# A fused hybrid decoder layer on one core: two of four input-weight sums of the second feed-forward made in DRAM, all DRAM sums paced

## The chip, the cores and the metric

The kernel runs on one core of one Trainium2 chip. The metric is the device time of one launch in microseconds (us), the median of the runs shown. A core has five engines that run their own instruction streams in order and wait for each other by semaphores: TensorE (PE, matmuls), VectorE (DVE), ScalarE (ACT), GpSimd (POOL) and SyncE (SP, which here only issues transfers). Transfers are carried by 16 DMA engines; those that SP issues are in one queue (q1 in the profile), those that GpSimd issues, accumulating ones among them, in another (q0).

## The reference, cut to what matters

```
def reference(x, mem, ...):
    x = x + 0.5 * swiglu(rms_norm(x, norm_ffn1_w), ffn1_w_in, ffn1_w_out)
    x = x + hybrid_mixer(rms_norm(x, norm_mix_w), ...)      # SSD heads and differential attention
    x = x + memory_cross_attention(rms_norm(x, norm_cross_w), rms_norm(mem, norm_mem_w), ...)
    x = x + 0.5 * swiglu(rms_norm(x, norm_ffn2_w), ffn2_w_in, ffn2_w_out)
    return rms_norm(x, norm_final_w)

def swiglu(h, w_in, w_out):
    gate, up = split(h @ w_in, 2)
    return (silu(gate) * up) @ w_out
```

x is 512 tokens by 1024 features in float32, the feed-forward width is 2816 = 22 tiles of 128, the memory has 256 rows. Everything is float32.

## The kernel before

**Precision.** Each float32 operand is split into a high and a low part (`wh` on ScalarE by a copy, `wl` on VectorE by a subtraction, lines L151 and L152), and each product is three matmuls: high by high, high by low, low by high. The activations lie with features on partitions in the tiles `x[0..7]`.

**Block products.** Most of both feed-forwards is multiplied by a scheme of seven block products in place of eight (Winograd's form of Strassen's). It needs sums of blocks of the weights. `quad` makes two tiles each of gate and up outputs from four weight blocks of 128 x 1024 (512 KB), called b11, b12, b21, b22. It uses seven weight operands in this order: m1 = b11, t = b12 + b11, t2 = t + b22, m2 = b21, m7 = b12 + b22, m3 = b22, t4 = t2 + m2. Each of the seven is one call of `add_product`, 24 matmuls of 256 columns, into one of three accumulators in PSUM, named qa, qe and qb. Between products ScalarE copies accumulators (qb<-qa at L267, u<-qb at L277), and TensorE waits for these copies before it adds into qb again.

**How the sums are made.** In the first feed-forward VectorE adds t2 and t4 in SBUF. In the second one (`by_transfer`), SP loads a block into a raw tile `wr` and GpSimd issues a transfer that adds another block to it: t gets b11 from DRAM, t2 gets the finished tile t from SBUF, m7 gets b22 from DRAM. t4 is added by VectorE. The raw tiles have six buffers, the split ones three each.

**The output weights of the second feed-forward** are used in the same way by `out_blocks`: the work is cut into three parts (`THIRDS`: 8, 8 and 6 tiles of the width), each with its input quads (4, 4 and 3) and then seven block products into the accumulators oa, oe and ob, 24 or 18 matmuls of 512 columns each. Its four sums of blocks are made in DRAM, in the tensors `wsum`: SP copies a block to `wsum` (1 MB, or 768 KB for the last part), and GpSimd adds another one to it in slices of 512 KB. The generator `out_sums` issues this between the instructions of the mixer, 60 us of planned TensorE time after the first feed-forward ends.

**Order of the work.** The program is generated by Python generators: the dense matmuls run as one stream, and side work (attention heads, SSD groups, sums) is spawned as chains that become ready when a count of planned TensorE time (`od.t`) passes; `yield 5.0` means 5 us of it. SP's stream keeps this program order exactly. The streams of the other engines are ordered by a scheduler at build time. SP waits for a free `wr` buffer at each weight load, so its stream runs some five weight tiles ahead of TensorE.

**SSD groups.** Each of four groups (`group`) loads rows of cumulated decays, `r<-cum_d` (L790), by GpSimd, four of 256 KB; ScalarE and VectorE turn them into masked decays (L848 to L852), and TensorE multiplies them into `py`.

**The end.** After the last part's products, `update` adds them to the tiles x (now turned to tokens on partitions), and `final` makes the last norm: squares of both halves of a token block (junk, L1187), multiplication by the norm's weight (`gain`), a power on GpSimd (frr, L1193), a scaling, and two output transfers by SP. The norm's weight is loaded by SP ahead of the last part's output weights.

Of the kernel before, what the change touches and what calls it, by code (L numbers as in the profile page):

```python
# [11 lines left out]
F32 = mybir.dt.float32  # L12
R32 = mybir.dt.float32r
AF = mybir.ActivationFunctionType
ALU = mybir.AluOpType
# [81 lines left out]
def body(tc, a, dbg=None):  # L97
# [38 lines left out]
    last, start, last_sum, recent = [], [], [], []  # L136
# [111 lines left out]
    def quad(xs, src, by_transfer):  # L248

        b12, b11, b22, b21 = src[0], src[1], src[2], src[3]
        m1, t = raw_w(b11), raw_w(b12, b11)
        if by_transfer:
            t2, m2, m7, m3 = raw_w(b22, t), raw_w(b21), raw_w(b12, b22), raw_w(b22)
            t4 = m2
        else:  # L260
            m3, m2, m7 = raw_w(b22), raw_w(b21), raw_w(b12, b22)
# [5 lines left out]
        S.activation(b_ps, a_ps, AF.Copy)  # L267
# [3 lines left out]
        if not by_transfer:  # L271
            V.tensor_tensor(t2, t, m3, ALU.add)
        yield from add_product(b_ps, split_w(t2), xs, S2, False)
        if not by_transfer:
            V.tensor_tensor(t4, t2, m2, ALU.add)
        u2 = s2("u2")
        S.activation(u2, b_ps, AF.Copy)  # L277
# [123 lines left out]
    def ffn_quads(xs, wq, st, nq, made, places, by_transfer=False):  # L401

        for _ in range(nq):
            for out in quad(xs, next(wq), by_transfer):
                if out is None:
                    yield
# [372 lines left out]
    def group(g, bt, ct, xs, zs):  # L779
# [13 lines left out]


# [46 lines left out]
        for j in range(2):  # L841
# [235 lines left out]

    wsum = [[dram.tile([P, nf // 2 * T], F32, name=f"wsum{c}{t}") for t in range(4)] for c, (_, nf) in enumerate(THIRDS)]

    def out_sums():  # L1080
        for t, (to, of) in enumerate(((B12, B11), (B12, B22), (B22, 0), (B21, 2))):
            for c in range(len(THIRDS)):
                blocks = a[f"f2b{c}"]
                nc.sync.dma_start(wsum[c][t], blocks[to])
                yield 5.0
                more = wsum[c][of] if t > 1 else blocks[of]
                for k in range(0, more.shape[1], D):
                    ks = slice(k, min(k + D, more.shape[1]))
                    G.dma_start(wsum[c][t][:, ks], more[:, ks], accum_op=ALU.add)
                    yield 3.0  # L1090

    def out_blocks(c, g, col4, last):
# [37 lines left out]
        def update(tb, half_, src):  # L1130
            V.scalar_tensor_tensor(x[4 * half_ + tb], src, col4[:, tb : tb + 1], x[4 * half_ + tb], ALU.mult, ALU.add)  # L1131

# [35 lines left out]
        for t in range(2):  # L1168
            update(t, 1, e_ps[t])
            if last is not None:  # L1170
                last(t)
        for t, m in enumerate([product(b_ps, sums[3], "22", by_pair=last is not None)]):
            yield from m
        for t in range(2):
            update(t + 2, 0, b_ps[t])
            if last is not None:
                last(t + 2)

    def ffn2():
        wq = iter(a["f2q"])  # L1180
        col4, gain = None, []

        def final(tb):
            ss = small("fss", 2)
            for n in range(2):
                junk = s2("junk")
                S.activation(junk, x[4 * n + tb], AF.Square, accum_out=ss[:, n : n + 1])  # L1187
# [11 lines left out]
        for c, (_, nf) in enumerate(THIRDS):  # L1199
            g = []  # L1200
            yield from ffn_quads(xs_2, wq, st_2, nf // 2, block_tiles(g), BY_BLOCK, True)
# [102 lines left out]
```

## Time and profile before

| | |
|---|---|
| runs | 1382.34 us median of 3 (1377.25 to 1385.79) |
| the profiled execution | 1377.29 us, of which the instructions' span is 1375.3 us |
| granted TensorE clock | 0.985 mean |
| TensorE matmul busy | 1319.3 us (96%), 7766 recorded |
| VectorE, ScalarE, GpSimd busy | 978.0 us (71%), 667.3 us (49%), 135.0 us (10%) |
| moved | 211.17 MB; SP's queue 35.3% of the 16 engines' span, GpSimd's 20.4% |

Rough stages by time from the span's start: first feed-forward to 366 us, mixer to some 850 us, cross-attention to some 978 us, second feed-forward to the end. Its three parts have their quads at 978 to 1072, 1110 to 1199 and 1238 to 1311 us.

How to read it: a row of the timeline gives the start, the duration, engine, line, operation, tile written <- tiles read, and in square brackets the time that the engine stood idle before it and what ended that. In the table of waits the three numbers are the sum in us, the count and the longest. In the table by windows PEclk is the granted TensorE clock and DMA share the busy share of the 16 DMA engines.

### The profile page before, as it was taken

To read this page: it belongs to the slowest core of one execution; us is meant where nothing else is said; L and a number is where in the kernel's file an instruction comes from. 1 tells how busy PE (TensorE), PEld (TensorE's weight loads), DVE (VectorE), ACT (ScalarE), POOL (GpSimd) and SP (SyncE) were. 2 spreads that over 40 slices of the span, in tenths; PEclk is the share of its full clock that TensorE was granted. 3 is DMA by queue.
4 is the path that set the end of the run, shared out by engine and by line. 5 is a ranking of instruction groups with operands and counts; after the bars stand their busy time and mean duration, and the time that the engine had idled before them with its cause. 6 is when DMAs were issued, how large, how long until landed. Compare 5 with 4: busy or idle time off the path is not lost. (4 is left out here: it accounts for less than half of the span.)

```text
span 1375.3 us, 20006 instructions
## 1 busy us (share of the span) xinstructions
PE 1319.3 (96%) x7766; PEld 1145.8 (83%) x7766; DVE 978.0 (71%) x1533; ACT 667.3 (49%) x1124; POOL 135.0 (10%) x158
## 2 busy tenths in 40 slices
PE   8999999999999998999999999999999999999973
PEld 7888999799888787877888878888899899889862
DVE  6875778477875775657777786566978777876854
ACT  5442445155454563446654574344565544554543
POOL 1000010100122111200101110000110011001000
PEclk9999999999999999999999999999999999999987
DMA  7434576365489738721264473221677688768622
GB/s 262 109 121 123 132 205 237 90 175 151 142 287 242 211 85 160 239 91 55 37 149 85 102 182 114 92 63 55 144 189 209 199 230 200 199 191 238 186 76 84
DMA packets 62047, 211.17 MB, mean 154 GB/s; under 512 B 7880, under 2 KB 10416, under 8 KB 61760
## 3 DMA queue, kind: packets, MB, share of 16 engines
q1 hardware_dynamic: 47904, 162.62, 35.3%
q0 software_dynamic: 14048, 47.27, 20.4%
q8 instruction: 61, 1.00, 0.3%
q14 instruction: 34, 0.28, 0.1%
HBM read 201.94 MB, written 27.84 MB: 167 GB/s over the span
## 5 line engine op out<-in xcount | busy, mean ns | idle before, releaser
L151 ACT ACTIVATE wh<-wr 128x1024 fp32r<-128x1024 f32 (+2 forms) x311 | 316.0, 1020 | 378.2 <-issue 81.2
L152 DVE TENSOR_TENSOR wl<-wr,wh 128x1024 fp32r<-128x1024 f32 (+2 forms) x311 | 365.8, 1179 | 147.3 <-ACT wh L151 142.8
L142 PE MATMUL po<-gh,wh 128*128 128x512 f32 x176 | 68.8, 392 | 0.0
L142 PE MATMUL po<-gl,wh 128*128 128x512 f32 x176 | 68.5, 390 | 0.0
L142 PE MATMUL po<-gh,wl 128*128 128x512 f32 x176 | 68.4, 389 | 0.0
L231 PE MATMUL qa<-hmh,wl 128*128 128x256 f32 x216 | 61.2, 283 | 0.8 <-DVE wl L152 0.8
L231 PE MATMUL qa<-hml,wh 128*128 128x256 f32 x216 | 61.1, 283 | 0.0
L231 PE MATMUL qa<-hmh,wh 128*128 128x256 f32 x216 | 61.1, 283 | 0.0
L231 PE MATMUL qb<-s31h,wh 128*128 128x256 f32 x152 | 44.4, 292 | 8.4 <-ACT u L277 8.4
L142 PE MATMUL pxbc<-hnh,wh 128*128 128x512 f32 x128 | 52.3, 408 | 0.0
L142 PE MATMUL pxbc<-hnl,wh 128*128 128x512 f32 x128 | 50.2, 392 | 0.0
L142 PE MATMUL pxbc<-hnh,wl 128*128 128x512 f32 x128 | 50.2, 392 | 0.0
L666 ACT ACTIVATE ec<-ec,mn 128x512 f32<-128x512 f32 (+3 forms) x64 | 35.4, 555 | 29.3 <-DVE mn L665 29.3
L239 POOL DMA_DIRECT2D wr<-in_f2q x22 | 19.0, 862 | 295.3 <-DMA wr<-in_f2q 89.7
L231 PE MATMUL qb<-s24h,wh 128*128 128x256 f32 x152 | 44.4, 292 | 3.6 <-ACT qb L267 3.5
L231 PE MATMUL qe<-s31h,wh 128*128 128x256 f32 x152 | 44.0, 290 | 1.7 <-ACT wh L151 1.7
L231 PE MATMUL qe<-s31h,wl 128*128 128x256 f32 x152 | 43.8, 288 | 0.8 <-DVE wl L152 0.8
L231 PE MATMUL qe<-s31l,wh 128*128 128x256 f32 x152 | 43.9, 288 | 0.2 <-DVE s31l L152 0.2
L231 PE MATMUL qb<-s24l,wh 128*128 128x256 f32 x152 | 43.7, 288 | 0.0
L231 PE MATMUL qb<-s24h,wl 128*128 128x256 f32 x152 | 43.7, 287 | 0.0
L474 DVE TENSOR_TENSOR upd<-po,row 128x512 f32<-128x512 f32 x24 | 16.6, 690 | 38.1 <-PE po L142 38.0
L231 PE MATMUL qb<-s31h,wl 128*128 128x256 f32 x152 | 43.6, 287 | 0.0
(436 smaller groups left out, 4132.0 us busy)
## 6 DMA issues: line engine op xcount, KB each, us to landing
wr<-in_f2q SPq DMA_DIRECT2D x66, 512.0 KB, 4.8
wr<-in_f1q SPq DMA_DIRECT2D x40, 512.0 KB, 4.2
wr<-in_f2q POOLq DMA_DIRECT2D x22, 512.0 KB, 7.9
wr<-wsum SPq DMA_DIRECT2D x20, 512.0 KB, 4.2
wr<-in_f1q POOLq DMA_DIRECT2D x16, 512.0 KB, 5.9
wr<-in_f1o SPq DMA_DIRECT2D x16, 512.0 KB, 4.3
wr<-in_wxbc SPq DMA_DIRECT2D x16, 512.0 KB, 4.2
wr<-in_f2b SPq DMA_DIRECT2D x15, 512.0 KB, 3.9
```

What stands on the lines that cost most here:

```text
L142: nc.tensor.matmul(out, w, x, start=start, stop=stop)
L151: S.activation(hi, src, AF.Copy),
L152: V.tensor_tensor(lo, src, hi.bitcast(F32), ALU.subtract),
L231: nc.tensor.matmul(out, a_[:, wc], b_, start=first and f == 0 and kp == 0 and j == 0, stop=kp == n - 1 and j == 2, skip_group_check=True)
L239: last_sum[:] = [G.dma_start(raw, m, accum_op=ALU.add).ins]
L474: V.tensor_tensor(upd, po, row4, ALU.mult)
L666: S.activation(ec[:, :n], ec[:, :n], AF.Exp, bias=mn, scale=-1.0, accum_out=sm[c][:, i : i + 1])
```

## The change

Three things change.

1. For each of the 11 quads of the second feed-forward, t and t2 are made in DRAM (`isum`) during the mixer and cross-attention; `quad` loads them as it loads a plain block. Of the three adding transfers of a quad only m7's is left. The split of m7 and the addition of t4 change places in the code.
2. `block_sums_in_dram` takes the place of `out_sums`. It makes the sums of both kinds in one list of 46 jobs, part by part, in pieces of 512 KB: a copy by SP, and two jobs later the adding transfer by GpSimd, some 10 us of planned time a job, from 10 us after the first feed-forward. It issues nothing while a group stands in `hold`: from the group's start until its second pair of decay rows is in use.
3. The last norm is taken half by half: each update of a half is followed by that half's square and multiplication, and the second to come only adds. Its weight is loaded by GpSimd.

```
-    def quad(xs, src, by_transfer):
+    def quad(xs, src, ready):
...
-        m1, t = raw_w(b11), raw_w(b12, b11)
-        if by_transfer:
-            t2, m2, m7, m3 = raw_w(b22, t), raw_w(b21), raw_w(b12, b22), raw_w(b22)
+        m1 = raw_w(b11)
+        if ready:
+            t, t2, m2, m7, m3 = raw_w(ready[0]), raw_w(ready[1]), raw_w(b21), raw_w(b12, b22), raw_w(b22)
             t4 = m2
...
-        w2 = split_w(m2)
-        if by_transfer:
+        yield from add_product(a_ps, split_w(m2), xs, "12", False)
+        w7 = split_w(m7)
+        if ready:
             V.tensor_tensor(t4, t2, m2, ALU.add)
-        yield from add_product(a_ps, w2, xs, "12", False)
-        yield from add_product(b_ps, split_w(m7), xs, S3, False)
+        yield from add_product(b_ps, w7, xs, S3, False)
...
-            od.spawn(out_sums(), 60.0)
+            od.spawn(block_sums_in_dram(), 10.0)
...
+        hold.append(g)
...
+            if j == 1:
+                hold.remove(g)
...
-    def out_sums():
-        for t, (to, of) in enumerate(((B12, B11), (B12, B22), (B22, 0), (B21, 2))):
-            for c in range(len(THIRDS)):
-                blocks = a[f"f2b{c}"]
-                nc.sync.dma_start(wsum[c][t], blocks[to])
-                yield 5.0
...
-                    G.dma_start(wsum[c][t][:, ks], more[:, ks], accum_op=ALU.add)
-                    yield 3.0
+    def block_sums_in_dram():
+        jobs = []
+        for c, (f0, nf) in enumerate(THIRDS):
+            gs = range(f0 // 2, (f0 + nf) // 2)
+            jobs += [(isum[g][0], a["f2q"][g][0], a["f2q"][g][1]) for g in gs]
+            jobs += [(isum[g][1], a["f2q"][g][2], isum[g][0]) for g in gs]
...
+        for n in range(len(jobs) + 2):
+            while hold:
+                yield 1.0
+            if n < len(jobs):
+                nc.sync.dma_start(jobs[n][0], jobs[n][1])
+                yield 4.0
+            while hold:
+                yield 1.0
+            if n > 1:
+                G.dma_start(jobs[n - 2][0], jobs[n - 2][2], accum_op=ALU.add, max_dma_last_dim=4 * D)
+                yield 6.0
...
-        def final(tb):
-            ss = small("fss", 2)
-            for n in range(2):
-                junk = s2("junk")
-                S.activation(junk, x[4 * n + tb], AF.Square, accum_out=ss[:, n : n + 1])
-                V.tensor_tensor(x[4 * n + tb], x[4 * n + tb], gain[n], ALU.mult)
-            v = small("fv", 1)
-            V.tensor_tensor(v, ss[:, 0:1], ss[:, 1:2], ALU.add)
-            V.tensor_scalar(v, v, 1.0 / D, EPS, ALU.mult, ALU.add)
+        def final(tb, n):
+            xt, ss, junk = x[4 * n + tb], small("fss", 1), s2("junk")
+            S.activation(junk, xt, AF.Square, accum_out=ss)
+            v = small("fv", 1, bufs=6)
+            if tb not in sq:
+                V.tensor_scalar(v, ss, 1.0 / D, EPS, ALU.mult, ALU.add)
+            else:
+                V.scalar_tensor_tensor(v, ss, 1.0 / D, sq[tb], ALU.mult, ALU.add)
+            V.tensor_tensor(xt, xt, gain[n], ALU.mult)
...
-                    nc.sync.dma_start(gain[n], a["final"][n].partition_broadcast(P))
+                    G.dma_start(gain[n], a["final"][n].partition_broadcast(P))
```

Three places where the streams differ. Numbers behind a name count the tiles and differ between the builds.

GpSimd's stream at the start of the second feed-forward, in the kernel before: per quad three adding transfers, into t, into t2 (from the tile t in SBUF) and into m7.

```order
L239 DMA wr_10169<-in_f2q 128x1024
L239 DMA wr_10172<-wr_10169 128x1024
L239 DMA wr_10177<-in_f2q 128x1024
L239 DMA wr_10421<-in_f2q 128x1024
L239 DMA wr_10424<-wr_10421 128x1024
L239 DMA wr_10429<-in_f2q 128x1024
```

The same place in the changed kernel, from the last sums of output weights on: one adding transfer per quad, into m7.

```order
L1104 DMA wsum_272<-wsum_271 128x1024
L1104 DMA wsum_272<-wsum_271 128x512
L239 DMA wr_9677<-in_f2q 128x1024
L335 TENSOR_TENSOR ncol_9743<-nv_9741,mhalf 128x4
L346 TENSOR_TENSOR ndiag_9842<-ident,cl_9836 128x512
L239 DMA wr_9951<-in_f2q 128x1024
L239 DMA wr_10249<-in_f2q 128x1024
```

The adds into t and t2 have left this place and stand as `isum` rows in the mixer and in cross-attention. GpSimd's stream around the decay rows of the first SSD group, in the kernel before (rr is the norm of an attention head):

```order
L724 TENSOR_TENSOR rr_4990<-ev_4987,mhalf 128x4
L724 TENSOR_TENSOR rr_5198<-ev_5195,mhalf 128x4
L1089 DMA wsum_242<-wsum_241 128x1024 x2
L790 DMA r_5383<-cum_d 128x4x128
L790 DMA r_5385<-cum_d 128x4x128
L790 DMA r_5462<-cum_d 128x4x128
L790 DMA r_5464<-cum_d 128x4x128
L1089 DMA wsum_246<-wsum_245 128x1024 x2
```

And in the changed kernel:

```order
L724 TENSOR_TENSOR rr_5019<-ev_5016,mhalf 128x4
L724 TENSOR_TENSOR rr_5226<-ev_5223,mhalf 128x4
L1104 DMA wsum_264<-wsum_263 128x1024
L790 DMA r_5407<-cum_d 128x4x128
L790 DMA r_5409<-cum_d 128x4x128
L790 DMA r_5485<-cum_d 128x4x128
L790 DMA r_5487<-cum_d 128x4x128
L1104 DMA wsum_264<-wsum_263 128x1024
L1104 DMA isum_247<-in_f2q 128x1024
```

One add stands ahead of the decay rows in place of two; its copy on SP was issued two jobs earlier. ScalarE's stream at the end of the last input quad, where the last part's output products begin, in the kernel before (u is the copy ahead of the fifth product, th the gate's tanh, g11h to s24h the splits of the gate's result, the last four rows splits of output weights):

```order
L277 ACTIVATE u_2513_12855<-qb_12795 128x512
L151 ACTIVATE wh_12945<-wr_12758 128x1024
L412 ACTIVATE th_12974<-gate_12973 128x1024
L151 ACTIVATE g11h_12985<-th_12974 128x256
L151 ACTIVATE gh_12981<-th_12974 128x512
L151 ACTIVATE s31h_12994<-s_2529_12989 128x512
L151 ACTIVATE s24h_12998<-s_2530_12990 128x512
L151 ACTIVATE wh_13014<-wr_13012 128x1024
L151 ACTIVATE wh_13032<-wr_13030 128x1024
L151 ACTIVATE wh_13050<-wr_13048 128x512
L151 ACTIVATE wh_13062<-wr_13060 128x512
```

And in the changed kernel:

```order
L277 ACTIVATE u_2513_12911<-qb_12851 128x512
L151 ACTIVATE wh_13001<-wr_12814 128x1024
L151 ACTIVATE wh_13070<-wr_13068 128x1024
L151 ACTIVATE wh_13088<-wr_13086 128x1024
L151 ACTIVATE wh_13106<-wr_13104 128x512
L412 ACTIVATE th_13030<-gate_13029 128x1024
L151 ACTIVATE wh_13118<-wr_13116 128x512
L151 ACTIVATE g11h_13041<-th_13030 128x256
L151 ACTIVATE gh_13037<-th_13030 128x512
L151 ACTIVATE wh_13136<-wr_13134 128x1024
L1167 ACTIVATE ob_13066<-oa_13062 128x512
```

The splits of the first output weights have moved ahead of the gate of the last quad; the splits s31h and s24h now stand behind the copies of oa to ob. TensorE's stream is the same but for two places: at this one, the first product into ob begins before the last matmuls into oe, and near the end of the mixer two `py` matmuls stand a few rows later. VectorE's stream moves as ScalarE's does at the end of the last quad. In all other quads the streams of VectorE and ScalarE are the same as before.

More of the change, by code (lines that the diff above doesn't have):

```diff
@@ L399, in gated, with ffn_quads @@
         return gate
-    def ffn_quads(xs, wq, st, nq, made, places, by_transfer=False):
+    def ffn_quads(xs, wq, st, nq, made, places, sums=None):
         for _ in range(nq):
-            for out in quad(xs, next(wq), by_transfer):
+            for out in quad(xs, next(wq), next(sums) if sums else None):
                 if out is None:
@@ L1075, in turn @@
             yield 3.0
+    isum = [[dram.tile([P, D], F32, name=f"isum{g}{t}") for t in range(2)] for g in range(NF // 2)]
     wsum = [[dram.tile([P, nf // 2 * T], F32, name=f"wsum{c}{t}") for t in range(4)] for c, (_, nf) in enumerate(THIRDS)]
-    def out_sums():
-        for t, (to, of) in enumerate(((B12, B11), (B12, B22), (B22, 0), (B21, 2))):
-            for c in range(len(THIRDS)):
-                blocks = a[f"f2b{c}"]
-                nc.sync.dma_start(wsum[c][t], blocks[to])
-                yield 5.0
[L1086 to L1089, printed above, removed]
-                    yield 3.0
+    def block_sums_in_dram():
[4 more added lines that the diff above has]
+            jobs += [(isum[g][1], a["f2q"][g][2], isum[g][0]) for g in gs]
+            blocks, sums = a[f"f2b{c}"], wsum[c]
+            for t, (to, more) in enumerate(((blocks[B12], blocks[B11]), (blocks[B12], blocks[B22]), (blocks[B22], sums[0]), (blocks[B21], sums[2]))):
+                for k in range(0, nf // 2 * T, D):
+                    ks = slice(k, min(k + D, nf // 2 * T))
+                    jobs.append((sums[t][:, ks], to[:, ks], more[:, ks]))
+        for n in range(len(jobs) + 2):
[9 more added lines that the diff above has]
+                yield 6.0
     def out_blocks(c, g, col4, last):
@@ L1131, in update @@
             V.scalar_tensor_tensor(x[4 * half_ + tb], src, col4[:, tb : tb + 1], x[4 * half_ + tb], ALU.mult, ALU.add)
+            if last is not None:
+                last(tb, half_)
         bank = [acc, aux]
```

23 lines of the change are left out of this document (11 added, 12 removed).

## The prediction

> **What bounds the kernel now.** The page says that TensorE is busy 96% of the span, so only its waits can be won. The table of TensorE's waits, read first, has five that matter:
>
> ```profile
> PE ob L1115 <- ACT wh L151: 12.0, 1, 12.0
> PE oa L1115 <- ACT wh L151: 9.0, 1, 9.0
> PE qb L231 <- ACT u L277: 8.4, 8, 2.6
> PE py L142 <- DVE r L852: 5.1, 2, 3.8
> PE qb L231 <- ACT qb L267: 3.5, 4, 1.7
> ```
>
> That is 38.0 us. Two are single waits in the last 70 us, two belong to the quads, one to an SSD group. The change touches the causes of all five. I take them in turn, each with the timeline at its place.
>
> **The quads of the second feed-forward.** The longest wait among them, at 1197, read backwards over GpSimd, ScalarE and TensorE:
>
> ```profile
> 1176.76 0.86 POOL L239 DMA_DIRECT2D wr<-wr  x1 [6.40 <-DMA wr<-in_f2q]
> ...
> 1184.97 1.06 ACT L151 ACTIVATE wh<-wr 128x1024 fp32r<-128x1024 f32 x1 [4.01 <-DMA wr<-wr]
> ...
> 1196.41 0.59 ACT L277 ACTIVATE u<-qb 128x512 f32<-128x512 f32 x1
> ...
> 1197.05 0.39 PE L231 MATMUL qb<-s31h,wh 128*128 128x256 f32 x1 [2.58 <-ACT u L277]
> ```
>
> TensorE waits for the copy u, which is no slow copy: ScalarE had stood for 4.01 us at t2's split, whose add from SBUF (wr<-wr) was issued only when t's own add had landed, 6.40 us late. So two adds in a chain are the cause, and ScalarE's stream hands the delay on. Three further waits follow a late split of t2, and the windows show what the pauses do to the clock:
>
> ```profile
> 1144.46 0.39 PE L231 MATMUL qb<-s24h,wh 128*128 128x256 f32 x1 [1.74 <-ACT qb L267]
> 1153.06 0.39 PE L231 MATMUL qb<-s31h,wh 128*128 128x256 f32 x1 [1.09 <-ACT u L277]
> 1280.05 0.38 PE L231 MATMUL qb<-s31h,wh 128*128 128x256 f32 x1 [2.57 <-ACT u L277]
> ...
> 1138.00:1152.00 14.00, 12.22 (x88) 11.81 (x86) 9.90 (x14) 7.64 (x11) 0.86 (x1) 0.88 0.74 161
> 1192.00:1206.00 14.00, 11.42 (x94) 11.19 (x93) 11.19 (x15) 6.39 (x9) 0.00 (x0) 1.00 0.56 188
> 1276.00:1290.00 14.00, 11.43 (x83) 11.23 (x82) 10.17 (x13) 5.70 (x8) 1.72 (x2) 0.88 0.89 240
> ```
>
> With `isum` both adds leave this place: t and t2 come as plain loads by SP, in the same number as before. The four waits are 2.58 + 1.74 + 1.09 + 2.57 = 8.0 us. In two of the three windows the granted clock was 0.88, so 0.12 x 14 = 1.7 us were lost in each, 3.4 in both. Gain 11.4. The other 3.9 us of the two rows (8.4 + 3.5 - 8.0) I leave: they come from ScalarE's order, which is the same in these quads.
>
> The Trainium skill, "TensorE: Matmul & The Clock Gate", Part 1, says that the clock halves after at least one idle window of about 3.4 us and that this window runs free. By it pauses of 2.6 us would cost no clock, and the term would be 8.0 and the time 3.4 us higher. The trace decides otherwise for 1280 and agrees for 1197: of two equal pauses one lowered the clock and one did not.
>
> What is late next is m7, the one operand that still takes an add:
>
> ```profile
> 1123.16 1.06 ACT L151 ACTIVATE wh<-wr 128x1024 fp32r<-128x1024 f32 x1 [1.50 <-DMA wr<-in_f2q]
> ...
> wr<-in_f2q POOLq DMA_DIRECT2D x22, 512.0 KB, 7.9
> ```
>
> ScalarE has waited 1.50 us for it with q0 full. The 7.9 us of the last row is the median landing of such adds beside two others per quad; alone in q0 it should be quicker. Bounds: nothing, or 0.8 us in each of ten quads, 8. I take 1.0, since the one wait shown was swallowed by ScalarE's slack. Quads: 11.4 - 1.0 = 10.4 us.
>
> **The start of the last output part.**
>
> ```profile
> 1312.14 1.06 ACT L412 ACTIVATE th<-gate 128x1024 f32<-128x1024 f32 x1 [8.83 <-DVE gate L411]
> 1315.28 0.42 ACT L151 ACTIVATE g11h<-th 128x256 fp32r<-128x256 f32 x1 [2.08 <-DVE th L415]
> ...
> 1319.26 2.51 ACT L151 ACTIVATE wh<-wr 128x1024 fp32r<-128x1024 f32 x3
> ...
> 1321.61 4.52 PE oa L1115 x10
> ...
> 1328.87 1.36 PE oa L1115 x6
> ```
>
> The first weight split runs at 1319.26, behind the whole gate chain of the last quad, though its data had landed. TensorE needs no gate of that quad for the first 24 matmuls (two products over the two earlier quads). After the pause ten matmuls took 4.52 us where six took 1.36, so 0.45 against 0.227 each: 2.25 us of clock. In the changed order these splits stand ahead of the gate, and 24 x 0.227 = 5.4 us of work fill the pause; at some 1316.5 g11h (1315.28) is there. What remains of the wait lies between nothing and 9.0 - 5.4 = 3.6: the splits s31h and s24h now stand behind the two copies of oa. I take 1.9, near the middle, as neither end has a row nearer. Gain 9.0 + 2.25 - 1.9 = 9.4.
>
> **The end.** After the sixth product SP sends out two token blocks and only then loads the last sum:
>
> ```profile
> 1354.34 4.37 DMA wr<-wsum
> ...
> 1359.93 0.80 PE L1115 MATMUL ob<-wh,gh 128*128 128x512 f32 x1 [12.02 <-ACT wh L151]
> ...
> L1187 ACT ACTIVATE junk<-x x8: 612/615/633, 1342.8 to 1367.7; 128x512 f32<-128x512 f32 x8
> L1187 ACT ACTIVATION_READ_ACCUMULATOR junk<-x x8: 185/187/188, 1343.3 to 1368.2; 128x1 f32 x8
> ```
>
> SP's order there has not changed: four outputs, then the load. So the wait of 12.02 stays but for what the norm's chain loses: one square of 0.615 + 0.187 and one addition of 0.15, before the outputs at 1352 and again at the very end. 2 x 0.95 = 1.9 us, between nothing and 3. The weight of the norm on GpSimd I cost at nothing: that engine has no work there but the four powers.
>
> **The SSD group.**
>
> ```profile
> 523.18 1.72 POOL L1089 DMA_DIRECT2D wsum<-wsum  x2 [7.53 <-DMA wsum<-in_f2b]
> 524.30 3.68 POOL L790 DMA_DIRECT2D r<-cum_d  x4
> ...
> 541.11 0.63 ACT L848 ACTIVATE e<-r 64x512 f32<-64x512 f32 x1 [4.33 <-DMA r<-cum_d]
> ...
> 544.62 0.69 PE L142 MATMUL py<-r,xdt 128*64 128x128 f32 x2 [3.78 <-DVE r L852]
> 546.62 1.97 PE L142 MATMUL py<-r,xdt 128*64 128x128 f32 x14 [1.31 <-DVE r L852]
> ...
> 540.00:554.00 14.00, 8.91 (x42) 6.99 (x41) 8.47 (x14) 8.87 (x23) 0.00 (x0) 0.76 0.92 240
> ```
>
> GpSimd stood 7.53 us for a copy to land before it could issue the decay rows. Now that copy is issued two jobs, some 20 us of planned time, ahead of its add, and nothing else is issued meanwhile. Rows issued 7.5 us earlier let the second e run at 533.6 and the second pair of matmuls at 539.1, ahead of 540.84 when TensorE first stood still. Gain 3.78 + 1.31 of wait and 0.24 x 14 = 3.4 of clock, 8.5 at most, nothing at least; I take 8.0.
>
> **What the change adds.** 22 copies and 22 adds of 512 KB between 366 and 978.
>
> ```profile
> 366.00:560.00 194.00, 188.17 (x1035) 153.24 (x1034) 134.37 (x296) 98.36 (x227) 36.77 (x40) 0.98 0.75 200
> 560.00:978.00 418.00, 417.51 (x2150) 343.21 (x2149) 291.37 (x522) 210.94 (x423) 42.96 (x47) 1.00 0.40 103
> ...
> q1 hardware_dynamic: 47904, 162.62, 35.3%
> q0 software_dynamic: 14048, 47.27, 20.4%
> ...
> 370.94 1.96 POOL L335 TENSOR_TENSOR ncol<-nv,mhalf 128x4 f32<-128x4 f32 x1 [60.08 <-DVE nv L333]
> ```
>
> In q1 1375.3 x 0.353 / 162.62 MB makes 1.6 us of all engines per 512 KB, in q0 3.1. A copy both reads and writes DRAM, so it may cost 1.6 to 3.1; 44 transfers come to 103 to 136 us over 612, a share of some 0.2. The DMA share there was 0.75 at first, with the sums of output weights crowded into it, and 0.40 later; spreading them evens this out to some 0.7. TensorE was busy 417.51 of 418 us, and weight loads run five tiles ahead: that hides the transfers. Uncovered is GpSimd's stream: three adds now stand ahead of ncol at 370.94, on which the mixer's norm waits, each about 1 us to issue. I take 3 us; the lower end is nothing, the upper 15.3, if the adds put the decay rows of the three other groups late as they did the first's (5.1 each).
>
> **The sum.** Against the profiled execution: 1377.3 - 10.4 - 9.4 - 1.9 - 8.0 + 3.0 = 1350.6, rounded 1350. This execution stands at the low end of the runs shown, 5 us below their median of 1382.34, so the runs of the changed kernel may lie a few us above the sum as well.
>
> **The rivals.**
> - *m7 becomes the bound of the quads.* For it speaks the 1.50 above, against it the empty q0. It costs the upper end, 7 us more: 1357.
> - *The decay rows stay late*, because an add of 512 KB still stands right ahead of them in q0 and the four rows land one after the other: the gain of 8.0 is lost, 1358.
> - *The mixer pays for the traffic:* the upper end of 15.3 in place of 3, 1362. The Trainium skill, "DMA: Bandwidth & Descriptors", section "Issuing engines are not separate DMA queues", says that transfers of all issuers share the same 16 engines and interleave; it speaks for this rival. The window at 540, with a DMA share of 0.92 just where TensorE stood, is in line with it.
> - *Slower: GpSimd stands at its adds.* Before, it has waited long for copies that SP issued late:
>
> ```profile
> POOL wsum L1089 <- DMA wsum<-in_f2b: 109.2, 12, 28.3
> ```
>
> Twice as many pieces now pass through the same two streams. If copies come later than two jobs allow, head norms and group norms stand behind the adds. One wait of 28.3 us fell where nobody needed GpSimd; two such waits on work that TensorE needs at once give 1350 + 56.6 = 1407. It decides from the point where SP, held by a free weight buffer, issues a copy more than some 15 us after its place.
>
> **How the numbers follow.** Forecast 0.60 (its own range, from the bounds of its terms, 1342 to 1358), m7 0.10, decay rows 0.10, traffic 0.12, GpSimd 0.05, and 0.03 for a mishap at the end that leaves the time within 1%. A measurement of this kernel can tell about 1% from no change, that is 1368.5 to 1396. The first four stay below 1368.5 for the most part: faster 0.86, same 0.09, slower 0.05. The range goes from 1339, all gains at their full bound (11.4 + 11.25 + 3 + 8.5) and the 3.9 us of the quads as well, to 1370, the traffic rival with runs that lie as far above the profile as now.
>
> **What would show it.** Right: no wait of ScalarE for wr<-wr, and the rows qb <- u and qb <- qb at some 4 us together; oa waits under 4 us near 1290; py gone from TensorE's waits; ob still waits some 11; the DMA share near 0.6 from 560 to 978 and near 0.5 in the second feed-forward. Wrong: ScalarE waiting for wr<-in_f2q in most quads; TensorE waiting for nrow or for rows of the norm near 375; GpSimd waiting long for isum or wsum copies; any new wait of TensorE in the mixer.

## The result, and the profile after

The changed kernel takes 1400.16 us (median of 6 runs, 1396.56 to 1408.72) where the kernel before took 1378.22 beside it (6 runs, 1373.48 to 1385.79): a ratio of 1.0158, 95% interval 1.0119 to 1.0197. It is slower by 1.6%, and the prediction of 1350 us with a range up to 1370 is wrong. The profiled execution took 1396.56 us, its span is 1394.8 us. (Comparisons use undisturbed runs alone; where medians of separate comparisons are set side by side, their ratios to the kernel before are the better measure.)

TensorE's table of waits after the change, with the columns sum in us, count and longest, answers the five rows of before:

```profile
PE py L142 <- DVE r L853: 28.6, 7, 15.7
PE ob L1130 <- ACT wh L151: 11.6, 1, 11.6
PE pt L146 <- DVE mn L665: 5.4, 2, 2.7
PE qb L231 <- ACT u L277: 3.7, 8, 0.5
PE qb L231 <- ACT qb L267: 1.0, 2, 0.5
```

What was expected of the second feed-forward came: the waits of qb fell from 11.9 to 4.7 us and oa has no row any more. But py, which was to vanish, grew from 5.1 to 28.6, in seven waits, the longest 15.7. So the time went ahead of the second feed-forward. How much it was is read from two markers, TensorE's first matmul into qa of the second feed-forward and its first into oa of the last output part. These rows come from the timeline by tile (durations min/median/max, then first and last start), the two of before first, then those of after:

```profile
L231 PE MATMUL qa<-h11h,wh x32: 278/283/365, 989.1 to 1059.9; 128*128 128x256 f32 x32
L1115 PE MATMUL oa<-wh,g11h x6: 389/628/794, 1320.3 to 1329.4; 128*128 128x512 f32 x6
```

```profile
L231 PE MATMUL qa<-h11h,wh x18: 278/283/365, 1032.1 to 1079.9; 128*128 128x256 f32 x18
L1130 PE MATMUL oa<-wh,g11h x6: 389/389/396, 1342.9 to 1349.1; 128*128 128x512 f32 x6
```

The second feed-forward starts 43.0 us later (1032.1 against 989.1). From there to the last part it takes 310.8 us against 331.2, 20.4 less, and from there to the end of the span 51.9 against 55.0, 3.1 less. 1377.3 + 43.0 - 20.4 - 3.1 = 1396.8, the profiled 1396.6. Below, the start of qa stands for the mixer and cross-attention, and the stretch from qa to oa for the quads and the start of the last part.

The largest of the new waits, followed backwards over three engines. First TensorE's timeline, then GpSimd's, then SP's, and last a window that takes in most of the pause and its end (columns: length, busy time and count of PE, PEld, DVE, ACT, POOL, then the granted clock, DMA share and GB/s):

```profile
840.60 0.61 PE L142 MATMUL pcv<-wh,hm 128*128 128x512 f32 x2
856.94 0.69 PE L142 MATMUL py<-r,xdt 128*64 128x128 f32 x2 [15.73 <-DVE r L853]
...
834.85 0.93 POOL L1104 DMA_DIRECT2D wsum<-wsum  x1 [17.03 <-DMA wsum<-in_f2b]
835.46 1.91 POOL L790 DMA_DIRECT2D r<-cum_d  x2
...
824.72 2.54 SPq L1099 DMA_DIRECT2D wsum<-in_f2b  x1
...
844.00:858.00 14.00, 1.06 (x3) 0.73 (x4) 2.58 (x5) 5.29 (x14) 0.92 (x1) 0.51 0.76 118
```

py needs the second pair of decay rows of group 3. GpSimd issued them at 835.46, right behind an adding transfer for whose copy it had stood 17.03 us. SP issued that copy at 824.72, 10.1 us before the add. The granted clock of 0.51 in the last row is mostly that of the pause itself, since TensorE was busy for only 1.06 us of these 14; behind the pause the clock was 0.50 from 857 to 861 us and 0.94 from 861 to 865. By that the half clock added some 2 us to the 15.7 (an estimate: half of 4 us). So the decay rows stood behind an add. The order of GpSimd's instructions as built shows why (the columns are the place in its stream, the line, and what is written and read; `r` are decay rows of group 3, `wsum_268` the last block sum of the second part):

```
117 L790 DMA r_7903<-cum_d 128x4x128
118 L790 DMA r_7905<-cum_d 128x4x128
119 L905 DMA mem_8068<-in_memT 128x256
120 L1104 DMA wsum_268<-wsum_267 128x1024
121 L790 DMA r_7994<-cum_d 128x4x128
122 L790 DMA r_7996<-cum_d 128x4x128
```

In the program no add can stand there: the pauses (`hold`) let none out between a group's start and the use of its last rows. But only SP's stream keeps the program's order. GpSimd's is ordered by the build, and the build put the add ahead. Its table of waits after the change, where one row of before had 109.2 us:

```profile
POOL wsum L1104 <- DMA wsum<-in_f2b: 220.5, 24, 27.1
POOL isum L1104 <- DMA isum<-in_f2q: 147.0, 19, 45.7
```

### The profile page after: what moved, and what is told of

Same layout as the page of the kernel before. It is cut to its first block, busy times and chain, and to the rows that moved or that the text cites. A ratio compares the mean times of both kernels' runs of the same rounds, so it can differ in the third digit from the quotient of the medians.

```text
span 1394.8 us, 20038 instructions
## 1 busy us (share of the span) xinstructions
PE 1323.1 (95%) x7766; PEld 1146.3 (82%) x7766; DVE 977.0 (70%) x1533; ACT 668.7 (48%) x1124; POOL 134.4 (10%) x160
## 4 chain that ended last, share of the span: by engine, by line
PE 71%; DMA 10%; DVE 8%; issue 4%; ACT 3%; POOL 1%; SPq 0%; POOLq 0%; DVEq 0%; ACTq 0%
PE qb L231 10%; PE po L142 10%; PE qe L231 6%; PE pxbc L142 6%; PE pm L142 6%; PE qa L231 4%; DMA r<-cum_d 4%; PE ob L1130 3%; DVE wl L152 3%; PE pcq L142 3%; DMA wsum<-in_f2b 2%; PE pq L142 2%; PE oa L1130 2%; PE pz L142 2%; PE pk L142 2%
## 5 line engine op out<-in xcount | busy, mean ns | idle before, releaser
L665 DVE CUSTOM_DVE_ANT_0 ec<-ps,bias 128x512 f32<-128x512 f32 (+3 forms) x64 | 28.8, 487 | 25.6 <-DMA bias<-rel_z 17.8
L231 PE MATMUL qe<-s24h,wh 128*128 128x256 f32 x152 | 43.0, 283 | 0.0
L231 PE MATMUL qe<-s24l,wh 128*128 128x256 f32 x152 | 43.0, 283 | 0.0
```

The lines of the kernel that those rows point to most:

```text
L231: nc.tensor.matmul(out, a_[:, wc], b_, start=first and f == 0 and kp == 0 and j == 0, stop=kp == n - 1 and j == 2, skip_group_check=True)
L665: V.tensor_tensor_reduce(out=ec[:, :n], in0=ps[c][:, :n], in1=bias[:, T - n :], scale=0.125, scalar=3e38, op0=ALU.add, op1=ALU.min, accum_ ...
```

## The experiments

Theory A: the time is lost because the build moved adds ahead of decay rows, bias rows and norms on GpSimd, where they wait for copies that SP issues at their late place, while the rest stands behind. Rival B: the traffic of the sums delays the rows. The expectations speak of 44 copies and adds; the list in the code has 46.

**1. GpSimd in program order** (`e_pool`):

```
-    ctx.enter_context(tc.manual_schedule(engines={mybir.EngineType.SP}))
+    ctx.enter_context(tc.manual_schedule(engines={mybir.EngineType.SP, mybir.EngineType.Pool}))
```

> GpSimd's instructions are kept in the order in which the program writes them, as SP's already are; the same 44 copies and 44 adds of block sums are made, and nothing else differs from the changed kernel. In the changed kernel the add wsum_268 stands ahead of the second pair of decay rows of group 3, and wsum_264 and wsum_266 ahead of the rows of groups 0 and 1; here they stand behind them. Theory A (the time is lost because GpSimd stands in order at adds that were moved ahead of the decay rows, for copies that SP issues at their late place): the 28.6 us of py <- r fall below 8, the 6.8, 6.8 and 17.1 us of half clock at 619, 725 and 844 mostly go, and the time falls to 1350 to 1362. Rival B (the traffic of the sums itself delays the rows and the loads): the transfers are the same, so py stays near 28 us and the time between 1390 and 1400.

Measured: 1359.52 us (4 runs), ratio to the kernel before 0.9849 (0.9825 to 0.9872). The same transfers, another order on one engine, and 41 us are gone. Rival B as the only cause falls. From TensorE's waits:

```profile
PE qe L231 <- ACT wh L151: 6.8, 1, 6.8
PE py L142 <- DVE r L853: 1.7, 2, 1.4
```

py is down to 1.7. The new 6.8 us lie at 273 us in the first feed-forward: there an add for a quad's weights, which the build had put ahead of a norm's `ndiag`, now stood behind it. So program order everywhere is not best either.

**2. A longer lag between copy and add** (`e_lag6`):

```
-        for n in range(len(jobs) + 2):
+        for n in range(len(jobs) + 8):
...
-            if n > 1:
-                G.dma_start(jobs[n - 2][0], jobs[n - 2][2], ...)
+            if n > 7:
+                G.dma_start(jobs[n - 8][0], jobs[n - 8][2], ...)
```

> Each add is issued six copies behind its own copy instead of two; GpSimd's order is again left to the build, so adds still stand ahead of decay rows, and the transfers are the same in number and size. Theory A: the copies have landed when GpSimd comes to the adds, its 220.5 + 147.0 us of waiting for copies shrink below 60, rows are issued in time, and the time falls to 1350 to 1365. Rival B: same traffic, 1390 to 1400. A third possibility, that the adds cost GpSimd's rows their place in the queue of its transfers even without a wait: py stays above 15 us with GpSimd's waits gone, 1370 to 1385.

Measured: 1400.31 us, ratio 1.0141 (1.0112 to 1.0169), no gain at all; what I expected under A was wrong. GpSimd's waits and the same place of group 3:

```profile
POOL isum L1104 <- DMA isum<-in_f2q: 163.1, 17, 43.9
POOL wsum L1104 <- DMA wsum<-in_f2b: 135.7, 18, 17.6
...
840.49 0.93 POOL L1104 DMA_DIRECT2D isum<-in_f2q  x1 [16.91 <-DMA isum<-in_f2q]
841.09 1.92 POOL L790 DMA_DIRECT2D r<-cum_d  x2
```

An add stands ahead of the same pair of rows with nearly the same wait, and it is a later one of the list, the 35th where it was the 32nd. The waits for copies fell from 367.5 only to 298.8. The longer lag written in the program was used up by the build, which moved the adds further ahead.

**3. Adds or everything left out** (`e_noadds`, `e_none`, and `e_none` timed as `e_none_t`). The edits: the line of the adds is dropped; in the others that of the copies too, and single blocks are loaded in place of sums, so none of these kernels computes the layer. (The third expectation was written later than the other two; the 1354.5 us in it is the kernel of experiment 5.)

> The 44 adding transfers of the block sums are left out, so the sums are only copies of one block and the output is not the reference's; SP issues all 44 copies as before, and the second feed-forward loads the same tiles. GpSimd waits for no copy. Theory A: all of the loss in the mixer is gone, 1345 to 1358. Rival B: half of the transfers and a bit less than half of their time on the 16 DMA engines remain, so about half of the loss remains, 1370 to 1380.

> Neither copies nor adds: the second feed-forward loads single blocks where it would load sums (output not the reference's), with the same number and size of loads. This is the floor: what the changed second feed-forward would give if sums were free. Theory A: 1340 to 1350, at most 10 below the kernel without the adds, since copies cost TensorE little. Rival B: also 1340 to 1350, but 20 or more below the kernel without the adds.

> The kernel with neither copies nor adds of block sums (single blocks loaded in their place, output not the reference's), now timed against the kernel before. Its distance from the kernel with all adds behind GpSimd's earlier work (1354.5) is what 44 copies and 44 adds cost once nothing stands behind a late add. The prediction gave 3 with an upper bound of 15.3. By the profiles (waits of 4 us for bias rows and decay rows in the one, none in the other, and three short half-clock stretches) 5 to 9: 1345.5 to 1349.5. Rival, traffic free: 1352 to 1355.

Measured: 1345.61 and 1348.4 us (one run each), and 1346.67 us (4 runs), ratio 0.9746 (0.9718 to 0.9774). Copies alone, timed in one run, cost nothing that can be seen. Theory A's floor is right, and it is also the forecast's place: 1350.6 without the 3.0 for what the change adds is 1347.6.

**4. Adds behind the decay rows only** (`e_rows`), and only behind those of the last group (`e_one`). `rows` collects the rows' transfers; `behind` keeps what follows on an engine behind them, without a wait:

```
+                with behind(rows):                                   # e_one: rows if len(rows) == 16 else []
                     G.dma_start(jobs[n - 2][0], jobs[n - 2][2], ...)
```

> Only the adds are bound: none may stand ahead of decay rows that the program has issued before it; the rest of GpSimd's order (the first feed-forward's adds included) is left to the build as in the changed kernel. Transfers are the same. The kernel with all of GpSimd in program order lost 6.8 us at 273 us (qe <- wh, an add of the first feed-forward's weights behind ndiag) and about 5 us of clock with it, which are not there now. Theory A: 1346 to 1353. Rival B': that kernel's gain came from the order of something else on GpSimd (bias rows, norms), so that rows alone bring less than half of it: 1370 to 1385.

> As the kernel with adds behind the decay rows, but only for the adds written after the last rows of all (group 3: two adds of wsum_267, two of wsum_268); the adds ahead of the rows of groups 0 and 1 stay as in the changed kernel. It prices one hoist: the stall of 15.7 us at 840 and the half clock of 17.1 us behind it, so 15.7 + 17.1 / 2 = 24 us. Theory A: 1396.6 - 24 = 1373, give or take 4, with py <- r at 11 to 14 us. If the stalls are not additive (the core catches up later): 1380 to 1390.

Measured: `e_rows` 1376.75 us, ratio 0.9957 (0.9932 to 0.9982); `e_one` 1391.14 us, ratio 1.0078 (1.0043 to 1.0113), its profiled execution with a span of 1399.2 us well above that median. The rows alone bring 2.0% (1.0158 to 0.9957) of the 3.1% that program order brought (to 0.9849): the time lies in the rival's range, though the rival spoke of less than half. Freeing group 3 brings 0.8%, 11 us in place of 24, and both times given for `e_one` were too low. (A hoist is an add that the build moved ahead.) The 24 was too much from the start: most of the 17.1 us of half clock in it lay in the pause, as the window above shows, so this hoist cost some 18 us. TensorE's waits of `e_rows`, then of `e_one`, tell why:

```profile
PE pn L142 <- POOL ysq L882: 8.5, 2, 5.2
PE py L142 <- DVE r L853: 3.9, 2, 2.9
...
PE py L142 <- DVE r L853: 11.2, 7, 4.6
PE pn L142 <- POOL ysq L882: 4.2, 1, 4.2
```

The adds now stand behind the rows, and ahead of the next thing that GpSimd does for the group: its sum of squares `ysq`, for which the product `pn` waits.

**5. Adds behind all of GpSimd's earlier work** (`e_best`): `seen` collects every transfer and operation that the program gives GpSimd, and the adds are kept behind those; the first feed-forward is left to the build.

```
+                with behind(seen[-40:]):
                     G.dma_start(jobs[n - 2][0], jobs[n - 2][2], ...)
```

> The adds stand behind everything that the program has given GpSimd before them (decay rows, bias rows, the norms' powers and diagonals), while the first feed-forward's adds are ordered by the build. Theory A: as with the rows alone and some 3 us better, since the bias rows of the second pair of heads (5.4 us of pt <- mn and 2.2 of ps <- mn in the changed kernel) and nrow (2.1) come in time too: 1344 to 1350. If GpSimd's other work has slack: the same as with the rows alone, within 2 us.

Measured: 1354.54 us (6 runs), ratio 0.9799 (0.976 to 0.9838), 3.5% under the changed kernel and some 5 to 10 us above what I expected. GpSimd's waits for copies and sums, and the two markers:

```profile
POOL wsum L148 <- DMA wsum<-in_f2b: 12.4, 3, 8.5
POOL wsum L148 <- DMA wsum<-wsum: 9.2, 3, 4.7
POOL isum L148 <- DMA isum<-in_f2q: 4.2, 2, 2.3
...
L245 PE MATMUL qa<-h11h,wh x32: 277/283/365, 989.6 to 1060.5; 128*128 128x256 f32 x32
L1145 PE MATMUL oa<-wh,g11h x6: 389/389/396, 1300.5 to 1306.6; 128*128 128x512 f32 x6
```

That is 25.8 us of waiting in place of 367.5, with the lag of two jobs: that lag was long enough, in the order in which it was written. The second feed-forward starts at 989.6, 42.5 us earlier than in the changed kernel.

**6. The pauses left out**, from the changed kernel (`a_nohold`) and from `e_best` (`e_best_nohold`):

```
-            while hold:
-                yield 1.0
```

> The changed kernel without the pauses of the copies and adds at the decay rows. Theory A (the build's order on GpSimd decides, not the place in the program): adds stand ahead of decay rows and of head norms as before, and the time stays at 1390 to 1405. Rival (the pauses are at fault, since they push the copies late): 1365 to 1380.

> The kernel with all adds behind GpSimd's earlier work, without the pauses at the decay rows. Theory: with GpSimd's order kept, the pauses only keep two or three copies and adds out of each group; without them an add can stand ahead of decay rows in the program's own order, but its copy was issued two jobs before, so it waits little: 1352 to 1360. Rival (the pauses are needed: rows behind an add of 512 KB land late): 1362 to 1375, with py <- r above 5 us.

Measured: `a_nohold` 1383.68 us, ratio 1.0014 (0.9984 to 1.0045); `e_best_nohold` 1379.33 us, ratio 0.997 (0.9936 to 1.0004). So:

| | with pauses | without |
|---|---|---|
| GpSimd ordered by the build | 1.0158 | 1.0014 |
| adds kept in program order | 0.9799 | 0.997 |

Against the kernel with neither, the pauses alone lose 1.4%, the order alone gains 0.4% (the intervals of the two overlap), and both together gain 2.1%. Both times expected of `a_nohold` were missed. GpSimd waits there for copies as long as in the changed kernel, 188.9 + 175.6 = 364.5 us against 367.5, and yet the kernel is 1.4% faster: its build puts no add between the rows of group 3, which are issued at 813.47 and 815.51, and py waits 12.4 us in all, 7.6 at the longest, in place of 28.6 and 15.7. So it counts what stands behind a waiting add, and not how long GpSimd waits in sum.

With the order kept, leaving out the pauses costs 1.7%. That is the rival's direction, a little beyond its range, and rival B's mechanism, rows that land late, is seen for itself. TensorE's wait for py, GpSimd's timeline at group 3 and the first row of qa in `e_best_nohold`:

```profile
PE py L156 <- DVE r L867: 18.7, 11, 3.5
...
813.73 0.76 POOL L148 DMA_DIRECT2D r<-cum_d  x1 [0.86 <-PE nrow L156]
814.48 0.95 POOL L148 DMA_DIRECT2D isum<-isum  x1
815.06 0.94 POOL L148 DMA_DIRECT2D mem<-in_memT  x1
815.63 1.91 POOL L148 DMA_DIRECT2D r<-cum_d  x2
...
L245 PE MATMUL qa<-h11h,wh x24: 278/283/365, 1019.1 to 1069.0; 128*128 128x256 f32 x24
```

GpSimd waits for nothing of weight, yet py waits eleven times: the rows are issued in time and land late. The table of transfers gives the median from issue to landing of the 16 transfers of decay rows, for the kernel without sums, `e_best`, `e_best_nohold` and the changed kernel, in this order:

```profile
r<-cum_d POOLq DMA_DIRECT2D x16, 256.0 KB, 11.4
```

```profile
r<-cum_d POOLq DMA_DIRECT2D x16, 256.0 KB, 14.2
```

```profile
r<-cum_d POOLq DMA_DIRECT2D x16, 256.0 KB, 18.0
```

```profile
r<-cum_d POOLq DMA_DIRECT2D x16, 256.0 KB, 12.7
```

In the changed kernel they land quickly (12.7) and are issued late; in `e_best_nohold` they are issued in time and land late (18.0). The Trainium skill, "DMA: Bandwidth & Descriptors", section "Issuing engines are not separate DMA queues", says that all transfers share the same 16 engines and interleave; the step from 11.4 to 18.0 agrees with that. It does not show that sharing is the cause: whether the rows lose to the adds on the 16 engines or stand behind them in GpSimd's own queue is not separated here, and from 780 to 860 us the DMA share of `e_best_nohold`, 0.76, is not above that of `e_best`, 0.86.

**7. What the single gains are worth.** `b_rows` binds the adds of the kernel before behind its decay rows (as in 4). `e_sbuf` is `e_best` without isum: t and t2 of the quads are summed in SBUF again. `e_gain_sp` is `e_best` with the load of the last norm's weight back on SP.

```
-                    G.dma_start(gain[n], a["final"][n].partition_broadcast(P))
+                    nc.sync.dma_start(gain[n], a["final"][n].partition_broadcast(P))     # e_gain_sp
...
-            t, t2, m2, m7, m3 = raw_w(ready[0]), raw_w(ready[1]), raw_w(b21), raw_w(b12, b22), raw_w(b22)
+            t = raw_w(b12, b11)                                                          # e_sbuf
+            t2, m2, m7, m3 = raw_w(b22, t), raw_w(b21), raw_w(b12, b22), raw_w(b22)
```

> The kernel before, with its twelve adds of output weights bound behind the decay rows issued ahead of them in the program: two adds of wsum that stood ahead of the rows of group 0 stand behind them, nothing else moves. It prices the prediction's term for the SSD group by itself: py <- r at 540.8 and 544.6 (3.78 + 1.31 us) and the half clock of 6.8 us behind them go, so 1377 - 8 = 1369, ratio 0.994. Rival (what the adds hold back next, as in the changed kernel with the rows alone, where pn <- ysq took 8.5 us): the adds then stand ahead of group 0's sum of squares and TensorE waits there instead, ratio 0.998 to 1.003.

> The kernel with all adds behind GpSimd's earlier work, but t and t2 of the second feed-forward's quads are summed in SBUF again as in the kernel before, and the 22 copies and 22 adds of isum are left out. It prices what isum brings. By the prediction: quads + 10.4 and the start of the last output part + 9.4, less up to 3 for the traffic saved: 1354 + 17 to 20 = 1371 to 1374. Rival: the start of the last part owes its gain to other moves (the last norm by halves, its weight on GpSimd), so only the quads come back: 1362 to 1365.

> The kernel with all adds behind GpSimd's earlier work, with the two loads of the last norm's weight given back to SP. On ScalarE the first three weight splits of the last output part then stand behind th, g11h, gh, s31h and s24h of the last gate again, as in the kernel before. Theory: that load alone made the start of the last part late (SP holds it for a free buffer, and the weight loads queue behind it), so oa <- wh comes back with 8 to 9 us and 2 of clock: 1354.5 + 10 = 1364, give or take 2. Rival (another move of the change freed the start): 1353 to 1357.

Measured: `b_rows` 1384.82 us, ratio 1.0015 (0.9998 to 1.0032); `e_sbuf` 1363.79 us, ratio 0.9879 (0.9845 to 0.9912); `e_gain_sp` 1365.86 us, ratio 0.9885 (0.9841 to 0.9928). TensorE's waits in `b_rows`, the markers of `e_sbuf`, and a wait and the first oa of `e_gain_sp`:

```profile
PE pn L142 <- POOL ysq L879: 5.0, 1, 5.0
PE py L142 <- DVE r L852: 1.1, 1, 1.1
...
L245 PE MATMUL qa<-h11h,wh x32: 277/283/365, 986.5 to 1057.3; 128*128 128x256 f32 x32
L1144 PE MATMUL oa<-wh,g11h x6: 389/389/396, 1309.5 to 1315.7; 128*128 128x512 f32 x6
...
PE oa L1145 <- ACT wh L165: 9.0, 1, 9.0
L1145 PE MATMUL oa<-wh,g11h x6: 389/628/797, 1309.0 to 1318.5; 128*128 128x512 f32 x6
```

In `b_rows` pn waits 5.0 where py waited 5.1: the same adds, one place later. From qa to oa `e_sbuf` takes 323.0 us, `e_best` 310.9, the kernel before 331.2: isum is worth 12.1 of the 20.4, and the rest is the wait of oa, which does not come back without isum. The rival in the expectation of `e_sbuf` was right. The sums also make qa start 3.1 us later (989.6 against 986.5), so isum is worth some 9 us net. The wait of oa comes back, 9.0 us as before, when SP loads the norm's weight, and the time of `e_gain_sp` is as expected. So that load's place decides whether the last part starts late. The mechanism of the expectation, that the load holds SP's queue, is not what the trace shows: with it SP issues its first two loads of output weights at 1275.60 and 1278.43, without it (`e_best`) at 1276.28 and 1279.11. What changes is ScalarE's order as built: with the load on SP its first splits of that part stand behind the last gate again, from 1307.88, and without it ahead of it, from 1294.83.

**8. The end** (`e_best2`): the last weights are loaded and split ahead of the last updates and the four stores.

```
         yield from product(e_ps, blocks[B22], S4)
+        early = [weights(sums[3], part) for part in parts] if last is not None else None
         for t in range(2):
             update(t, 1, e_ps[t])
-        yield from product(b_ps, sums[3], "22", by_pair=last is not None)
+        yield from product(b_ps, sums[3], "22", by_pair=last is not None, ws=early)
```

> As the kernel before, and the last output part's last weights (two tiles of its fourth sum) are loaded and split ahead of the updates and of the four stores that SP issues before them. By the prediction's reading of the end (SP's order alone holds the load back) the 11.4 us of ob <- wh and the 10 us of half clock behind them go: 1330 to 1336. Rival: the splits need buffers of wh that the sixth product still holds, or ScalarE's squares are late instead: 1340 to 1350.

("The kernel before" in this text is `e_best`.) Measured: 1341.87 us (6 runs), ratio 0.9702 (0.9666 to 0.9737), 12.7 us below `e_best`, and the fastest here: 3.0% under the kernel before. TensorE's wait for `ob <- ACT wh` is gone from its table; what is left there is one row for ob:

```profile
PE ob L1145 <- DVE wl L166: 0.2, 1, 0.2
```

The time expected, 1330 to 1336, was missed, and the rival's range was right. The last matmul starts at 1329.81 in place of 1344.88, 15.1 us earlier, but the span ends only 12.2 earlier, so the work behind it takes 2.9 us longer; which part of it was not taken apart. The 10 us of half clock were again too much: in `e_best` the matmuls into ob start every 0.43 us, later every 0.23, and the slow ones last from 1337.65 to 1344.19, which costs some 3 us.

## Why the prediction was wrong, step by step

- *Quads, -10.4: right.* The waits for u and qb are 4.7 us, as foreseen, and isum brings 12.1 from qa to oa (experiment 7). The 1.0 set against it for m7 did not come.
- *Start of the last part, -9.4: right in size.* oa does not wait and runs at 389 ns where it ran at 628; the 1.9 left over for s31h and s24h is not there. The prediction read the new order but did not name the move behind it; it is the norm's weight on GpSimd (`e_gain_sp`), which the prediction had "cost at nothing". So the size rests on the stream that was read, and not on a cause that was named.
- *The end, -1.9: right in kind.* ob still waits 11.6. From oa to the end 3.1 us were won, of which 2.25 had been counted as clock at the start of the part, so about 0.9.
- *The SSD group, -8.0: did not come.* The step that failed is "Now that copy is issued two jobs, some 20 us of planned time, ahead of its add, and nothing else is issued meanwhile." That holds for the program and for SP, not for GpSimd. Here are the add right ahead of group 0's rows and SP's issue of its copy, first in the changed kernel, then in `e_best`:

```profile
527.71 0.94 POOL L1104 DMA_DIRECT2D wsum<-wsum  x1 [6.86 <-DMA wsum<-in_f2b]
522.57 0.50 SPq L1099 DMA_DIRECT2D wsum<-in_f2b  x1
...
517.89 0.88 POOL L148 DMA_DIRECT2D wsum<-in_f2b  x1
424.53 0.50 SPq L1113 DMA_DIRECT2D wsum<-in_f2b  x1
```

In the changed kernel it is the fifteenth add of the list, and its copy was issued 5.1 us before it, not some 20. In program order it is the twelfth, with a copy 93 us old and no wait. The term lacked a second step: `b_rows` frees the rows alone and gains nothing, because pn then waits. The size was about right for a kernel in which neither happens: without any sums qa starts 8.7 us earlier than before:

```profile
L231 PE MATMUL qa<-h11h,wh x32: 278/283/365, 980.4 to 1051.2; 128*128 128x256 f32 x32
```

- *What the change adds, +3.0 with an upper bound of 15.3: the term that failed by most.* Against 980.4 the changed kernel starts qa at 1032.1, 51.7 us later. With the adds in order (`e_best`, 989.6) it is 9.2, inside the bounds. That is what the adds cost in that order, since copies alone start qa at 981.1 (`e_noadds`); whether by their traffic or by the 25.8 us for which GpSimd still waits is not separated. The other 42.5 are the order on GpSimd, which the sum had no term for. The bound of 15.3 took three more groups at the 5.1 of the first; single waits of 15.7 and the half clock behind them were beyond it.
- *DMA shares.* Foreseen were about 0.6 in the mixer and 0.5 in the second feed-forward; the windows of the changed kernel give 0.64, 0.63 and 0.58 (the last one starts 34 us ahead of the second feed-forward; from 1032 to 1343 us the share is 0.60):

```profile
366.00:560.00 194.00, 186.05 (x1016) 150.73 (x1016) 131.48 (x293) 97.77 (x226) 29.16 (x33) 0.99 0.64 162
560.00:998.00 438.00, 406.59 (x2067) 332.66 (x2068) 272.83 (x491) 199.05 (x405) 62.92 (x72) 0.96 0.63 155
998.00:1335.00 337.00, 332.64 (x2312) 310.11 (x2312) 272.82 (x346) 185.99 (x238) 13.63 (x15) 1.00 0.58 169
```

- *The rivals.* "GpSimd stands at its adds" was given 0.05 and 1407, and it is what happened, at 1400. Its condition was wrong: SP was not late by its own order, the adds were early. What stood behind them was the decay rows above all, where it named norms. "The decay rows stay late" behind adds in flight is seen in `e_best_nohold`, at some 24 us (0.997 against 0.9799 of 1380). One add right ahead of the rows, which was its condition, is not enough: it stands ahead of groups 0 and 1 in `e_best` too, and py waits 1.9 us there in all. The place of "the mixer pays for the traffic" is the 9.2 us of `e_best`. In the changed kernel both lie under the larger loss.

The reading behind the chances can be named. The section on the change shows the add `wsum_264` right ahead of group 0's rows. An add stands there in program order too, but an earlier one of the list. The prediction took this one for an add whose copy had long landed, did not count its place in the list, and did not read the same place in the other three groups.

## What to carry to other kernels

Where only some engines keep the program's order, a pause or a lag written in the program binds only those: read what the build makes of the other end of each pair, and what stands behind it, before counting on it. An instruction that waits for a transfer belongs behind everything on its engine that must not wait, and that is its whole stream, not the one row that a profile names: the two repairs that moved adds behind the decay rows alone turned all or part of that wait into one for the next row. A good order and a pause can each be worth next to nothing or less alone (here a gain of 0.4%, within the noise, and a loss of 1.4%) and gain 2.1% together.

## What the runs showed of the hardware that was not expected

- Forty-six copies of 512 or 256 KB from DRAM to DRAM cost TensorE nothing that these runs can tell (1345.61 with them, in one run, and 1346.67 without). With the adds, kept in order, the decay rows landed later: in 14.2 us with pauses (13.0 in `e_gain_sp`, 14.7 in `e_pool`) and 18.0 without, in place of 11.4.
- The Trainium skill, "DMA: Bandwidth & Descriptors", section "Two DMAs through the same engine are not ordered", has the issuing engine wait on the first transfer's semaphore before it issues the second. The trace shows GpSimd waiting in this way, 17.03 us at one add and 367.5 us in the kernel. The price is set by the work behind the wait: 364.5 us of it in `a_nohold` went with a kernel that is 1.4% faster than the changed one.
- Behind the 15.7 us pause the granted clock was 0.50 from 857 to 861 us and 0.94 from 861 to 865. The pause cost more than its length, but only by some 2 us (estimated from these two windows), where the expectation of `e_one` had reckoned with half of 17.1.
